# Memory attention: the sample group's scores of four heads in four column groups, keys by batch

## The chip, the cores and the metric

The kernel runs on one core of a Trainium2 chip. Its time is the device time of one execution in microseconds (us), lower is better. Three runs of the kernel before are at hand, and one execution was profiled.

## What is computed

One inference step of a two-layer decoder, for a prompt of 512 tokens and for a sample group of 8 batches with 4 tokens each. Either layer is a mixer (layer 0: paged latent attention beside a state-space layer; layer 1: a gated recurrence), then a cross-attention into 256 memory tokens, then a squared-ReLU MLP, each with a residual. The change is in the cross-attention, whose reference is

```python
def mem_attend(hn, k, v, w_q, q_gain, w_o):
    b, L, _ = hn.shape
    q = rms_norm((hn @ w_q).reshape(b, L, MEM_HEADS, MEM_HEAD_DIM), q_gain)
    sc = jnp.einsum('bqhd,bkhd->bhqk', q, k).astype(jnp.float32) * (MEM_HEAD_DIM ** -0.5)
    pr = jax.nn.softmax(sc, axis=-1).astype(v.dtype)
    o = jnp.einsum('bhqk,bkhd->bqhd', pr, v).reshape(b, L, MEM_WIDTH)
    return o @ w_o
```

Here `hn` is the RMS-normalized residual (1024 features), with 4 heads of 128 features. The prompt's keys and values are computed from a memory; those of the sample group come from caches, 256 keys of 4 heads for each of the 8 batches and each layer. `rms_norm` divides by the root of the mean square plus 1e-6.

## The kernel before

The residual is kept feature-major, with 544 columns: 32 of the sample group, then 512 of the prompt. A dense product (`gemm`, helper `mm3`, line 190) takes 128 output features as a chunk, splits weights and activations into a high and a low part, and sums three products in two PSUM banks (`pbig`, two such pairs); four more banks (`psm`) serve everything small.

`mem_attention` runs once per layer. It begins with the layer norm's factor of each token: `rstd_cols` sums the squares in `acc` with a column of ones (tile `pst_m`), and `rstd_bcast` spreads the result over all partitions by products with the identity (`pbc_m`, `pbn_m`), into `rb`. Then comes the query projection, a `gemm` with one chunk for each head (`ps_mq`). Behind each chunk, `ev` multiplies by `rb` into `qT` (tile `mqT`), squares, and sums the squares for the head's own norm; a power on GpSimd makes the factor `r` from that sum plus 128 times the epsilon. The head's factor is applied later, as the scale of the softmax. `after` calls for each chunk the work that can follow: `head_scores` and `head_values` are the prompt's softmax and values, `sample_scores` the scores of the sample group.

`sample_scores(h)` masks the queries of the head, so that those of one batch stand alone in 32 columns (`mqp`). It loads the head's cached keys of four batches at a time (`mkc`, 512 KB), transposes them on TensorE, copies them out (`mkcT`), and multiplies: all eight batches accumulate in 32 rows of the PSUM tile `msS`, those of the head, with the weights in the head's group of 32 of the array's columns (`tile_position`). The rows are copied to `Ss`. Behind the last chunk come the sample group's softmax (`msP`, `msPT`), its values (`msO`: for each batch a load `mvc` of 512 KB, and eight products that go through the four column groups in turn), and the values of the prompt's heads (`mpt` transposes, `mpo` products). The output projection `ps_wmo` follows.

In layer 0 the steps of `fill` (tile `mkv`, with weights `w_mem_k` and `w_mem_v`) compute the other layer's memory keys and values between these; layer 1 has no such work left. `mkc` and `mvc` share the buffers of the tag `mc`, 5 in layer 0 and 8 in layer 1.

The order of the instructions on each engine is made by a planner: it takes instructions by the order of the program and by when, in its own model of the times, their inputs and buffers are ready. So work that stands later in the program is taken earlier where a hole would be. Loads go through the queue of SyncE (SP), in its order. At its head an instruction waits for its buffer, and those behind it wait too.

## Time and profile before

| what | value |
|---|---|
| median of three runs | 2033.66 us (2030.12 to 2038.61) |
| span of the profiled execution, first to last instruction | 2026.1 us |
| its own device time beside the span | not given with the profile; the median of the runs is 7.6 us above the span |
| TensorE matmul busy | 1974.1 us, 97% of the span |
| VectorE, ScalarE, GpSimd busy | 1250.1, 804.1 and 301.8 us |

The profile names an instruction by its line, engine, operation and tiles (out<-in). PE is TensorE, PEld its loading of weights, DVE VectorE, ACT ScalarE, POOL GpSimd, and SPq the queue of SyncE. An exact float32 product stands in the trace as two matmuls. The start of a matmul is recorded; its end is modelled, so that matmuls which follow each other overlap in the rows, and the time that one takes from the next is read from start to start.

### The profile page before, as it was taken

The numbers are of one execution on the slowest core, as the hardware profiler recorded it, in microseconds if no ns is written. First come the engines' busy times: TensorE is split into PE (matmuls) and PEld (weight loads), VectorE is DVE, ScalarE is ACT, GpSimd is POOL, SyncE is SP. The second block draws the span as 40 slices with busy tenths as digits, with TensorE's granted clock in tenths as the row PEclk, the third lists the DMA queues.
The fourth block names the chain that finished last, engine by engine and source line by source line (L and its number), as shares of the span: only waits on it lengthen the run. The fifth ranks groups of instructions, "written<-read, shape, count | busy, mean of one in ns | idle before, by whom it ended". The sixth has DMA issues, their size and how long they took to land.

```text
span 2026.1 us, 40767 instructions
## 1 busy us (share of the span) xinstructions
PE 1974.1 (97%) x16073; PEld 1848.0 (91%) x16073; DVE 1250.1 (62%) x2781; ACT 804.1 (40%) x1749; POOL 301.8 (15%) x400
## 2 busy tenths in 40 slices
PE   8999899999999999999999999999999999999999
PEld 7878699888899889999999999999898699999998
DVE  7988577877785455444434458888953553435353
ACT  4456655555654344222222334445342432212121
POOL 5677400000012112000000110011141010000000
PEclk9999989999999999999999999999989999999999
DMA  6110132122424533333232332323226132333232
GB/s 157 46 52 30 53 88 52 48 69 70 117 92 94 165 127 106 93 87 92 85 93 84 97 90 82 101 86 92 75 75 170 50 105 87 91 86 92 85 93 76
DMA packets 320480, 178.88 MB, mean 88 GB/s; under 512 B 49153, under 2 KB 312418, under 8 KB 320290
## 3 DMA queue, kind: packets, MB, share of 16 engines
q1 hardware_dynamic: 292466, 163.88, 28.2%
q10 hardware_dynamic: 26224, 8.06, 1.7%
q0 software_dynamic: 1600, 4.34, 0.8%
q8 instruction: 127, 2.08, 0.4%
q14 instruction: 63, 0.52, 0.1%
HBM read 166.42 MB, written 9.82 MB: 87 GB/s over the span
## 4 chain that ended last, share of the span: by engine, by line
PE 79%; SPq 3%; DVE 2%; issue 1%; DMA 1%; ACT 1%; POOL 0%; POOLq 0%; ACTq 0%; DVEq 0%
PE ps_dn L190 19%; PE ps_up L190 19%; PE kp L1110 6%; PE ps_wo L190 4%; PE hv L190 3%; PE ps_hq L190 3%; PE ps_hf L190 3%; PE ps_wmo L190 2%; PE ps_hg L190 2%; PE mkv L190 2%; PE ps_mq L190 2%; PE msS L1381 2%; SPq L1002 1%; SPq L976 1%; PE ct L300 1%
## 5 line engine op out<-in xcount | busy, mean ns | idle before, releaser
L190 PE MATMUL ps_up<-actH_f,wH_up 128*128 128x272 f32 x1024 | 211.9, 288 | 0.8 <-DVE mt L1458 0.8
L190 PE MATMUL ps_dn<-hidL,wH_dn 128*128 128x272 f32 x1024 | 211.7, 288 | 0.0
L190 PE MATMUL ps_up<-actH_f,wL_up 128*128 128x272 f32 x1024 | 210.5, 288 | 0.0
L190 PE MATMUL ps_dn<-hidH,wL_dn 128*128 128x272 f32 x1024 | 210.5, 288 | 0.0
L190 PE MATMUL ps_up<-actL_f,wH_up 128*128 128x272 f32 x1024 | 210.5, 287 | 0.0
L190 PE MATMUL ps_dn<-hidH,wH_dn 128*128 128x272 f32 x1024 | 210.0, 287 | 0.0
L1220 DVE TENSOR_TENSOR h<-ps_dn,h 128x544 f32<-128x544 f32 x64 | 46.4, 724 | 221.2 <-PE ps_dn L190 221.2
L165 ACT ACTIVATE wH_dn<-wraw_dn 128x1024 fp32r<-128x1024 f32 x64 | 68.1, 1063 | 255.1 <-PE ps_dn L190 157.9
L165 ACT ACTIVATE wH_up<-wraw_up 128x1024 fp32r<-128x1024 f32 x64 | 68.1, 1063 | 236.1 <-PE ps_up L190 142.7
L190 PEld LDWEIGHTS ps_up<-actH_f,wH_up 128*128 128x128 f32 x1024 | 159.5, 188 | 1.2 <-PE ps_up L190 1.1
L190 PEld LDWEIGHTS ps_dn<-hidL,wH_dn 128*128 128x128 f32 x1024 | 160.5, 188 | 0.1
L190 PEld LDWEIGHTS ps_up<-actL_f,wH_up 128*128 128x128 f32 x1024 | 160.0, 188 | 0.0
L190 PEld LDWEIGHTS ps_dn<-hidH,wL_dn 128*128 128x128 f32 x1024 | 159.5, 188 | 0.0
L190 PEld LDWEIGHTS ps_up<-actH_f,wL_up 128*128 128x128 f32 x1024 | 159.5, 188 | 0.0
L190 PEld LDWEIGHTS ps_dn<-hidH,wH_dn 128*128 128x128 f32 x1024 | 158.9, 188 | 0.0
L1458 DVE TENSOR_TENSOR mt<-ps_up,rb_f 128x544 f32<-128x544 f32 x64 | 46.2, 724 | 168.8 <-PE ps_up L190 168.6
L1113 ACT ACTIVATE sq<-kp 128x256 f32<-128x256 f32 x256 | 97.7, 386 | 77.8 <-PE kp L1110 47.9
L1116 DVE TENSOR_REDUCE ss<-sq 128x4 f32<-128x256 f32 x256 | 104.3, 412 | 13.3 <-ACT sq L1113 10.5
L166 DVE TENSOR_TENSOR wL_up<-wraw_up,wH_up 128x1024 fp32r<-128x1024 f32 x64 | 78.1, 1221 | 11.3 <-ACT wH_up L165 8.6
L1110 PE MATMUL kp<-wk0H,cH 128*128 128x256 f32 x256 | 79.8, 312 | 2.9 <-DVE S L1115 1.9
L166 DVE TENSOR_TENSOR wL_dn<-wraw_dn,wH_dn 128x1024 fp32r<-128x1024 f32 x64 | 78.2, 1222 | 5.8 <-ACT wH_dn L165 3.0
L1110 PE MATMUL kp<-wk0H,cL 128*128 128x256 f32 x256 | 72.7, 284 | 0.0
(734 smaller groups left out, 5227.1 us busy)
## 6 DMA issues: line engine op xcount, KB each, us to landing
wraw_up<-in_w_mlp_up_dram SPq DMA_DIRECT2D x64, 512.0 KB, 4.0
wraw_dn<-in_w_mlp_down_dram SPq DMA_DIRECT2D x64, 512.0 KB, 3.5
cnat<-in_cache_mla_latent_dram SPq DMA_DIRECT2D x128, 128.0 KB, 2.2
mkc<-in_cache_mem_k_dram SPq DMA_DIRECT2D x16, 512.0 KB, 7.3
mvc<-in_cache_mem_v_dram SPq DMA_DIRECT2D x16, 512.0 KB, 3.3
wraw_w_mem_k<-in_w_mem_k_dram SPq DMA_DIRECT2D x8, 512.0 KB, 5.4
wraw_w_mem_v<-in_w_mem_v_dram SPq DMA_DIRECT2D x8, 512.0 KB, 3.5
wraw_wo<-in_w_out_even_dram SPq DMA_DIRECT2D x8, 512.0 KB, 4.2
```

What stands on the lines that cost most here:

```text
L165: i = nc.scalar.activation(H, x, AF.Copy)
L166: sub.tensor_tensor(out=L, in0=x, in1=H.bitcast(F32), op=ALU.subtract)
L190: nc.tensor.matmul(out, x, sl(y), start=first and n == 0, stop=last and n == 2)
L300: self.nc.tensor.transpose(out, in_, self.ident[:p, :p])
L976: return [self.nc.sync.value_load(self.pt[0:1, b * NPG + t:b * NPG + t + 1], min_val=0, max_val=last) for t in range(NPG)]
L1002: load = lambda x, t, src: nc.sync.dma_start(x, src[bass.ds(pg[t], 1), 0].rearrange("o t c -> (o t) c"))
L1110: mm = nc.tensor.matmul(ps[:, :N], x[:, kt], wt[y][:, kt], start=(kt == 0 and n == 0), stop=(kt == 1 and n == 2))
L1113: nc.scalar.activation(sq, ps[:, :256], AF.Square)
L1116: V.tensor_reduce(out=ss[:, t, 4 * hf:4 * hf + 4], in_=sq.rearrange("p (h d) -> p h d", h=4), op=A, axis=AX.X)
L1220: self.nc.vector.tensor_tensor(out=halves(self.h[:, i, :]), in0=ps, in1=halves(self.h[:, i, :]), op=ALU.add)
L1381: nc.tensor.matmul(ps[32 * h:32 * h + 32, :MEM], qp[:, 4 * g + b, :], kcT[:, b, :], start=(g == b == 0), stop=(g == 1 and b == 3), tile_po ...
L1458: nc.vector.tensor_tensor(out=halves(t), in0=ps, in1=halves(rb), op=ALU.mult)
```

## The change

- `sample_scores` is split. `sample_keys(b)` loads the cached keys of one batch with all four heads (512 KB, runs of 2 KB) and transposes them into `mkcT`, of which there are 3 in layer 0 and 6 in layer 1 (`kbufs`). It is called for two batches behind each chunk as long as there are buffers, and for the other batches behind the projection.
- All score products stand behind the projection: for each batch four products, one for each head, in the four column groups. The masked queries of all heads are kept (`mqp`, 4 buffers). The softmax reads the PSUM tile itself, without `Ss`. `head_scores(2)` is called before the scores and no longer behind the softmax.
- The layer norm's factor is no longer applied to the queries, as the head's own norm cancels it but for the epsilon. `layer_norm` makes the epsilon term `en` of each token from the same sums of squares, and `rnorm` adds it. `rb` is gone; `ev` copies, and squares from PSUM.
- The shared buffers `mc` become 4 in layer 0 and 6 in layer 1. The square of the memory keys (`mksq`) takes a buffer of the tag `sq` in the filler.

The rest of the diff takes comments and docstrings out, which moves line numbers.

```diff
@@ -1282,7 +1282,9 @@
                 if wn == "w_mem_v":
                     break
                 for t in range(2):
-                    sq = p.tile([128, MH, MD], F32, name="mksq")
+                    sq = (self.tp.tile([128, NT], F32, tag="sq", name="mksq")[:, :MH * MD] if parts else
+                          p.tile([128, MH * MD], F32, name="mksq"))
+                    sq = sq.rearrange("p (h d) -> p h d", h=MH)
                     ss = p.tile([128, MH], F32, name="mkss")
                     nc.scalar.activation(sq, kr[:, t], AF.Square)
                     nc.vector.tensor_reduce(out=ss, in_=sq, op=ALU.add, axis=AX.X)
@@ -1296,7 +1298,7 @@
             nc.scalar.dma_start(o["mv_p"][l, 0].rearrange("(t p) h d -> p t (h d)", p=128), v)
 
     def mem_attention(self, l, act, acc, kv, P, fill):
-        """Returns the H and L parts of the attention output, feature-major (from P)."""
+
         nc, a = self.nc, self.a
         V, G = nc.vector, nc.gpsimd
         kT, v = kv
@@ -1304,31 +1306,50 @@
         oL = P.tile([128, MH, NT], F32R, name="moL")
         with self.pool(f"matt{l}", bufs=2, side="left") as p:
             qg = self.col(p, a["mem_q_gain"][l], MD, "g_mq2")
-            rb = self.rstd_bcast(self.rstd_cols(acc, D, f"m{l}"), f"m{l}")
             qT = p.tile([128, MH, NT], F32, name="mqT", bufs=1)
             sqs = p.tile([128, MH, NSAMP], F32, name="msqs", bufs=1)
-            Ss = p.tile([128, MEM], F32, name="msS", bufs=1)
-            # batch of each row (head, batch, position)
+
+
+            en = p.tile([128, TT], F32, name="men", bufs=1)
+            kcT, kbufs = {}, 6 if l else 3
+            qps = []
+
             bcol = p.tile([128, NB], F32, name="mbcol", bufs=1)
             V.tensor_reduce(out=bcol, in_=self.ident.rearrange("p (h b s) -> p b h s", h=MH, b=NB), op=ALU.add, axis=AX.XY)
             bm = self.c("bmask").rearrange("p (b n) -> p b n", b=NB)
             rs = []
 
-            def rnorm(ps, n):
+            def layer_norm():
+                ps = self.psm("pst")
+                for t in range(4):
+                    nc.tensor.matmul(ps[:, t:t + 1], acc[:, tok(t)], self.ones, start=True, stop=True)
+                accr = p.tile([128, MH, NSAMP], F32, name="maccr", bufs=1)
+                G.tensor_copy(accr, acc[:, None, :NSAMP].to_broadcast([128, MH, NSAMP]))
+                nc.tensor.matmul(ps[:, 4:5], accr.rearrange("p h n -> p (h n)"), self.ones, start=True, stop=True)
+                V.tensor_scalar(en, ps[:, :TT], MD * EPS / D, MD * EPS * EPS, op0=ALU.mult, op1=ALU.add)
+
+            def rnorm(ps, c, n):
                 r = p.tile([128, n], F32, name=f"mr{n}", bufs=4 if n > 1 else 1)
-                V.tensor_scalar(r, ps, MD * EPS, None, op0=ALU.add)
+                V.tensor_tensor(out=r, in0=ps, in1=en[:, c:c + n], op=ALU.add)
                 G.tensor_tensor(out=r, in0=r, in1=self.nhalf[:, :n], op=ALU.pow)
                 rs.append(r)
 
             def ev(i, ps):
-                V.tensor_tensor(out=halves(qT[:, i, :]), in0=ps, in1=halves(rb), op=ALU.mult)
+                V.tensor_copy(halves(qT[:, i, :]), ps)
                 sq = self.tp.tile([128, NT], F32, tag="sq", name="msq")
-                nc.scalar.activation(sq, qT[:, i, :], AF.Square)
+                nc.scalar.activation(halves(sq), ps, AF.Square)
                 G.tensor_copy(sqs[:, i, :], sq[:, :NSAMP])
+                if i == 0:
+                    layer_norm()
                 pss = self.psm("mss")
                 for t in range(4):
                     nc.tensor.matmul(pss[:, t:t + 1], sq[:, tok(t)], self.ones, start=True, stop=True)
-                rnorm(pss[:, :4], 4)
+                rnorm(pss[:, :4], 0, 4)
+                qp = p.tile([128, NB, 32], F32, name="mqp", bufs=MH)
+                V.scalar_tensor_tensor(out=qp, in0=qT[:, i, None, :NSAMP].to_broadcast([128, NB, 32]), scalar=qg,
+                                       in1=bm, op0=ALU.mult, op1=ALU.mult)
+                qps.append(qp)
+
             def head_scores(h):
                 r = rs[h]
                 S = self.pbig("mS")
@@ -1361,29 +1382,28 @@
                     nc.tensor.matmul(po, v[:, k, h * MD:(h + 1) * MD], PT[:, k, :], start=(k == 0), stop=(k == 1))
                 self.split(oH[:, h, NSAMP:], oL[:, h, NSAMP:], po)
 
-            # sample group: rows (head, batch, position)
-            def sample_scores(h):
-                qp = p.tile([128, NB, 32], F32, name="mqp")
-                V.scalar_tensor_tensor(out=qp, in0=qT[:, h, None, :NSAMP].to_broadcast([128, NB, 32]), scalar=qg,
-                                       in1=bm, op0=ALU.mult, op1=ALU.mult)
-                ps = self.psm("msS")
-                for g in range(2):
-                    kc = p.tile([128, 8, MD], F32, tag="mc", name="mkc", bufs=8 if l else 5)
-                    nc.sync.dma_start(kc, a["cache_mem_k"][l, 4 * g:4 * g + 4, :, h, :]
-                                      .rearrange("b (t p) d -> p (b t) d", p=128))
-                    kcT = p.tile([128, 4, MEM], F32, name="mkcT")
-                    for x in range(2):
-                        pk = self.psm("mkc")
-                        for y in range(4):
-                            self.transpose(pk[:, y * 128:(y + 1) * 128], kc[:, 4 * x + y, :])
-                        self.copy(kcT[:, 2 * x:2 * x + 2, :].rearrange("p x n -> p (x n)"), pk)
-                    for b in range(4):
-                        nc.tensor.matmul(ps[32 * h:32 * h + 32, :MEM], qp[:, 4 * g + b, :], kcT[:, b, :],
-                                         start=(g == b == 0), stop=(g == 1 and b == 3),
+
+            def sample_keys(b):
+                kc = p.tile([128, 2, MH * MD], F32, tag="mc", name="mkc", bufs=6 if l else 4)
+                kT_ = kcT[b] = p.tile([128, MH, MEM], F32, name="mkcT", bufs=kbufs)
+                nc.sync.dma_start(kc, a["cache_mem_k"][l, b].rearrange("(t p) h d -> p t (h d)", p=128))
+                for x in range(2):
+                    pk = self.psm("mkc")
+                    for y in range(2):
+                        h = 2 * x + y
+                        for t in range(2):
+                            self.transpose(pk[:, y * MEM + t * 128:y * MEM + t * 128 + 128],
+                                           kc[:, t, h * MD:(h + 1) * MD])
+                    self.copy(kT_[:, 2 * x:2 * x + 2, :].rearrange("p x n -> p (x n)"), pk)
+
+            def sample_scores(ps, b0, n):
+                for b in range(b0, b0 + n):
+                    for h in range(MH):
+                        nc.tensor.matmul(ps[32 * h:32 * h + 32, :MEM], qps[h][:, b, :], kcT[b][:, h, :],
+                                         start=(b == 0), stop=(b == NB - 1),
                                          tile_position=(0, 32 * h), skip_group_check=True)
-                self.copy(Ss[32 * h:32 * h + 32], ps[32 * h:32 * h + 32, :MEM])
-
-            def sample_softmax():
+
+            def sample_softmax(Ss):
                 st = p.tile([128, 3], F32, name="msst")
                 V.tensor_reduce(out=st[:, 0:1], in_=Ss, op=ALU.max, axis=AX.X, negate=True)
                 V.tensor_tensor(out=st[:, 0:1], in0=st[:, 0:1], in1=r_s, op=ALU.mult)
@@ -1402,7 +1422,7 @@
                 os = p.tile([128, MD], F32, name="mos", bufs=1)
                 for b in range(NB):
                     po = self.psm("msO")
-                    vc = p.tile([128, 2, MH * MD], F32, tag="mc", name="mvc", bufs=8 if l else 5)
+                    vc = p.tile([128, 2, MH * MD], F32, tag="mc", name="mvc", bufs=6 if l else 4)
                     nc.sync.dma_start(vc, a["cache_mem_v"][l, b].rearrange("(t p) h d -> p t (h d)", p=128))
                     for t in range(2):
                         for h in range(MH):
@@ -1420,7 +1440,9 @@
             def after(ch):
                 if ch > 1:
                     head_scores(ch - 2)
-                sample_scores(ch)
+                for b in (2 * ch, 2 * ch + 1):
+                    if b < kbufs:
+                        sample_keys(b)
                 if ch == 3:
                     head_values(0)
 
@@ -1428,11 +1450,18 @@
             self.gemm(a["w_mem_q"][l], KT, 0, MH, act, ev, f"mq{l}", after=after)
             pss = self.psm("mss")
             nc.tensor.matmul(pss[:, :1], sqs.rearrange("p h n -> p (h n)"), self.ones, start=True, stop=True)
-            rnorm(pss[:, :1], 1)
+            rnorm(pss[:, :1], 4, 1)
             r_s = rs[MH]
-            PT = sample_softmax()
+            head_scores(2)
+            ps = self.psm("msS")
+            for b in range(0, NB, kbufs):
+                n = min(kbufs, NB - b)
+                if b:
+                    for x in range(b, b + n):
+                        sample_keys(x)
+                sample_scores(ps, b, n)
+            PT = sample_softmax(ps[:, :MEM])
             next(fill, None)
-            head_scores(2)
             next(fill, None)
             head_values(1)
             next(fill, None)
```

## Rows read from the trace of the kernel before

**Rows 1.** The page: busy time of the engines; the ended-last chain by line.
```profile
PE 1974.1 (97%) x16073; PEld 1848.0 (91%) x16073; DVE 1250.1 (62%) x2781; ACT 804.1 (40%) x1749; POOL 301.8 (15%) x400
...
PE ps_dn L190 19%; PE ps_up L190 19%; PE kp L1110 6%; PE ps_wo L190 4%; PE hv L190 3%; PE ps_hq L190 3%; PE ps_hf L190 3%; PE ps_wmo L190 2%; PE ps_hg L190 2%; PE mkv L190 2%; PE ps_mq L190 2%; PE msS L1381 2%; SPq L1002 1%; SPq L976 1%; PE ct L300 1%
```

**Rows 2.** Windows: stretch, length, busy of PE, PEld, DVE, ACT, POOL, clock, DMA.
```profile
659.39:703.96 44.57, 44.19 (x319) 37.89 (x318) 16.71 (x32) 13.25 (x25) 7.83 (x9) 1.00 0.59 166
703.96:759.52 55.56, 55.27 (x468) 44.24 (x466) 34.53 (x73) 29.50 (x67) 7.76 (x7) 1.00 0.39 131
1521.32:1567.03 45.71, 44.34 (x319) 37.84 (x317) 17.21 (x32) 12.44 (x25) 7.93 (x9) 1.00 0.61 165
1567.03:1612.72 45.69, 41.81 (x320) 27.76 (x318) 22.36 (x54) 16.74 (x43) 1.88 (x3) 0.96 0.16 52
```

**Rows 3.** Waits of PE, 659:760, then 1521:1613: us in total, times, longest.
```profile
PE ps_mq L190 <- DVE mqT L1324: 0.4, 1, 0.4
...
PE msPT L300 <- ACT msP L1391: 1.3, 1, 1.3
PE ps_mq L190 <- DVE mqT L1324: 1.2, 1, 1.2
```

**Rows 4.** The chain in layer 0, in order of time: start, us, what.
```profile
682.18 1.84 PE msS L1381 x8
...
687.92 0.98 PE msS L1381 x4
```

**Rows 5.** Timeline of matmuls, then of weight loads, in the paged attention.
```profile
322.76 1.94 PE L1144 MATMUL pv<-cnat,Pm 128*32 128x257 f32 x32
324.63 0.62 PE L1146 MATMUL pv<-lat,Pm 32*32 32x257 f32 x2
...
322.76 1.46 PEld L1144 LDWEIGHTS pv<-cnat,Pm 128*32 128x32 f32 x32 [0.16 <-ACT sq L1113]
```

**Rows 6.** Timeline of PE in layer 0, the sample group's values.
```profile
738.09 1.95 PE L1409 MATMUL msO<-mvc,msPT 128*32 128x128 f32 x64
739.98 0.39 PE L190 MATMUL mkv<-wH_w_mem_v,memH 128*128 128x256 f32 x1
```

**Rows 7.** Timeline of PE in layer 0, the layer norm's spreading.
```profile
671.89 1.05 PE L276 MATMUL pbc_m<-ident,r_m 128*128 128x128 f32 x8
...
673.20 0.39 PE L190 MATMUL ps_mq<-actH_m,wH_mq 128*128 128x272 f32 x1
```

**Rows 8.** Timeline of DVE in layer 1, behind the last chunk.
```profile
1567.23 0.72 DVE L1324 TENSOR_TENSOR mqT<-ps_mq,rb_m 128x544 f32<-128x544 f32 x1 [0.50 <-PE ps_mq L190]
...
1568.47 0.48 DVE L1367 SCALAR_TENSOR_TENSOR mqp<-mqT,g_mq,ctab 128x256 f32<-128x256 f32 x1
```

**Rows 9.** Tile views of `mkc` and `mvc`: ns min/median/max, first and last start.
```profile
L1372 SPq DMA_DIRECT2D mkc<-in_cache_mem_k_dram x16: 368/1647/3838, 656.1 to 1530.9; - x16
...
L147 DVE COPY mkcT<-mkc x16: 684/692/692, 679.5 to 1581.0; 128x512 f32<-128x512 f32 x16
...
L1406 SPq DMA_DIRECT2D mvc<-in_cache_mem_v_dram x16: 367/368/445, 695.3 to 1581.5; - x16
```

**Rows 10.** Waits of SP's queue, 640:760.
```profile
SPq L1406 <- PE mkc L300: 20.1, 5, 6.7
```

**Rows 11.** The page, loads: engine, count, KB each, median us to landing.
```profile
mvc<-in_cache_mem_v_dram SPq DMA_DIRECT2D x16, 512.0 KB, 3.3
wraw_w_mem_k<-in_w_mem_k_dram SPq DMA_DIRECT2D x8, 512.0 KB, 5.4
```

**Rows 12.** Timeline of PE in layer 1's tail.
```profile
1585.20 1.12 PE L1361 MATMUL mpo<-mPT,mv 128*128 128x512 f32 x2
...
1590.56 2.07 PE L1361 MATMUL mpo<-mPT,mv 128*128 128x512 f32 x2 [0.58 <-ACT mPT L149]
...
1600.24 0.75 PE L190 MATMUL ps_wmo<-moH,wH_wmo 128*128 128x272 f32 x4
```

**Rows 13.** Groups by line: busy us, mean ns of one, idle before.
```profile
L1381 PEld LDWEIGHTS msS<-mkcT,mqp 128*32 128x32 f32 x128 | 11.8, 109 | 12.3 <-issue 1.2 <-ACT msq L1326 0.7 <-DVE mst L1339 0.3
```

## Prediction

> **What bounds the kernel now.** I read the page first: TensorE is busy for 1974.1 us, 97% of the span, and the chain that ended last is made almost wholly of TensorE lines; `msS`, the line that this change rewrites, is 2% of it [rows 1]. So TensorE's time is the kernel's time wherever TensorE has no hole. Has it holes at the two places that the change touches? The windows view, cut at the last matmul of each layer's query projection, answers. Layer 0 runs from 659.39 to 759.52, and TensorE is busy in 44.19 of 44.57 and in 55.27 of 55.56 us. Layer 1 runs from 1521.32 to 1612.72 and shows 44.34 of 45.71, then 41.81 of 45.69 us at a mean clock of 0.96 [rows 2]. Layer 0 is limited by TensorE alone (it has the other layer's memory keys and values, tile `mkv`, as filler); layer 1 nearly so, with 3.9 us of waits in its tail behind the projection. The waits view names the waits: in layer 0 0.4 us for `mqT`; in layer 1 1.2 us for `mqT` and, the longest of the tail, 1.3 us for `msP` [rows 3].
>
> **Sample scores.** Each of the 32 products of a layer is recorded as two matmuls of 256 columns, 64 in all. Today one head's products follow each other in one group of 32 columns of the array. In the chain a run of 8 takes 1.84 us, a run of 4 0.98 [rows 4]: 0.215 for each further matmul, about 0.12 for going in and out. Layer 0 has 3 runs of 8 and 10 of 4, 3 x 1.84 + 10 x 0.98 = 15.3 us; layer 1 has 2 and 12, 15.4 us.
>
> Afterwards consecutive products go to the four column groups in turn. No row has this product in that order, but two have its like. `pv` rotates the groups with 257 columns: 32 matmuls from 322.76 to 324.63, 1.87 us, 0.058 each [rows 5]. `msO` rotates with 128 columns: 64 from 738.09 to 739.98, 0.030 each [rows 6]. `pv` is the nearest: 64 x 0.058 = 3.7 us a layer in one run. If each batch stands alone, there are seven breaks more at 0.12, 4.5 us. I take 3.8. **Gain 11.6 us a layer, bounds 10.8 and 11.7.**
>
> The weight loads could speak against it. In the `pv` run 32 loads are done in 1.46 us, inside the 1.87 us of the matmuls [rows 5], so they add nothing there. The Trainium skill ("TensorE: Matmul & The Clock Gate", Part 3, "The mechanism") states that a weight load overlaps matmuls in flight only when it goes to another row group. Here all four groups use the same rows, and by that rule the loads would stand in the open; the `pv` rows disagree.
>
> **Layer norm of the queries.** Today `pst_m` (10 matmuls) feeds `r_m`, which 10 more matmuls, `pbc_m` and `pbn_m`, spread over the partitions, from 671.89 to 673.20: 1.3 us a layer [rows 7]. The first chunk's evacuation waits for that, and so does the third chunk's bank: the 0.4 and 1.2 us for `mqT` [rows 3]. All of this goes. The new `layer_norm` has ten matmuls in the place of those of `pst_m`: nothing. Its copy on GpSimd and its step on VectorE are hidden by the projection, in which these engines are busy for 7.8 and 16.7 of 44.6 us [rows 2]; without that cover a wait like today's, 1.2 us. **Gain 1.7 us in layer 0, 2.5 in layer 1.**
>
> **Evacuations.** The multiply by `rb` becomes a copy of the same size, the square reads the bank instead of `qT`, and four copies of `msS` and two of `rb` a layer are gone: nothing on TensorE, which works on beside them. It matters behind the last chunk. Today `mqT`, a weight part and `mqp` follow from 1567.23 to 1568.95, 1.7 us [rows 8]; afterwards they stand ahead of all scores, since no batch can be scored before head 3's queries are there. So what moves is this: today half of the `msS` runs lie inside the projection, then none does. TensorE has other work meanwhile (prompt heads, key transposes, in layer 0 the filler).
>
> **Keys by batch.** The transposes and copies are as many as before. The loads keep their 512 KB but with runs of 2 KB, as `mvc` has them: an issue takes SP 0.37 instead of 1.65 us [rows 9], 10 us a layer less in its queue. Against that, the buffers that `mkc` and `mvc` share fall from 5 to 4 in layer 0 and from 8 to 6 in layer 1, and only 3 or 6 transposed batches fit. In layer 0 keys 3 to 7 can be copied only after scores have freed a buffer, so behind the projection; the value loads wait for key buffers, and behind them in SP's queue stand the weights of `mkv` and `wmo`, for which the filler waits. SP's value loads wait 20.1 us for `mkc` already [rows 10], yet TensorE has 0.3 us of idle in that stretch [rows 2], because the filler covers it. New waits of layer 0: from 0 to 4 us (one load that starts when it is needed, 0.37 of issue and 3.3 to land [rows 9, 11]); I take 1.
>
> In layer 1 the value loads 6 and 7 can start only when values 0 and 1 have been used, behind the softmax of the samples, where today all eight are there. Two prompt heads' values can stand beside them, each with two `mpo` pairs of 1.1 us [rows 12] and its transposes. The tail loses cover, too: of its 41.8 us of work 7.7 are `msS` (6 runs of 4, 1 of 8), and 3.8 come back. It also pays a spell at the lower of the two clock levels: the pair of `mpo` at 1590.56, behind a wait of 0.58, takes 2.07 us, where the pair at 1585.20 takes 1.12 [rows 12]. The mean of 0.96 over 45.69 us is 3.7 us at half the clock, 1.8 us lost. New waits of layer 1: from 0 to 6 us (today's 3.9 a second time, and one such spell more); I take 3, near the middle, because TensorE still has 41.8 - 7.7 + 3.8 = 37.9 us of work there against a sample chain of 21 us: 1.7 of evacuation, 3.8 of scores, 0.7 for the last key copy [rows 9], and the 15.0 us that pass today from the end of `msS` at 1585.20 to the first `wmo` matmul at 1600.24 [rows 12].
>
> **The sum.** Layer 0: 11.6 + 1.7 - 1 = 12.3. Layer 1: 11.6 + 2.5 - 3 = 11.1. Together 23.4 us. What follows either place runs at TensorE's pace and simply comes earlier. The profiled execution's span is 2026.1 us; what lies around it is not in the page, and the median of the three runs, 2033.66, is 7.6 above it. Span 2026.1 - 23.4 = 2002.7, time 2002.7 + 7.6 = **2010.3 us**. With the bounds: the low score cost, no new wait and the old clock spell gone, 2 x 11.7 + 4.2 + 1.8 = 29.4, time 2004; the high score cost and all new waits, 2 x 10.8 + 4.2 - 10 = 15.8, time 2018.
>
> **The rivals.**
> - Waits eat half (0.15). One layer overruns its bound: layer 0 uses its filler up early, or the tail of layer 1 goes by its chains, 5 us more. For it: SP's long waits and fewer buffers. Against it: 99% busy in layer 0. Gain 10 to 16 us, 2018 to 2023.
> - The columns don't run side by side, with the loads in the open (0.02). A load of `msS` has 0.109 us [rows 13]; 64 add 7.0 us to the 3.8, so the gain is 4.6 a layer instead of 11.6: 2 x 4.6 + 4.2 - 4 = 9.4, 2024. The rotating runs speak against it [rows 5, 6]. This is what the rule cited above would give (the Trainium skill, "TensorE: Matmul & The Clock Gate", Part 3, "The mechanism").
> - No change that shows (0.10). Each layer gets one new wait as long as the gain: the first value product waits for its load, which stood behind a key buffer. SP's longest such wait is 6.7 us [rows 10], and two loads behind each other take 6.6, 13.3 in all. For it: only a freed buffer starts a value load. Against it: `msO` comes 34 us behind the projection in layer 0. Time 2024 to 2044.
> - Slower (0.05). SP's queue is in order: value loads that wait for key buffers stand ahead of the weights of `mkv`, the filler cannot start, and TensorE stops in layer 0 behind the scores. From 23.4 us of such a stop on, the kernel is slower; all eight weight loads behind it, 5.4 us each for those of the keys [rows 11], are 43 us, less the gain 20, 2053.
>
> The rest, 0.68, is the forecast with its bounds, 2004 to 2018. A change under 0.5% (10 us) can't be told from none in this kernel, whose three runs span 8.5 us. Faster by more: 0.68 + 0.15 = 0.83; within: 0.02 + 0.10 = 0.12; slower: 0.05. Eight times in ten: 2004 to 2021, which leaves out the last three rivals and the worst of the first.
>
> **What would show it.** In the new profile: `msS` in runs of 8 or more at about 0.06 us each, 3.8 us a layer; no `pbc_m` or `pbn_m`; layer 0 from the first `ps_mq` to the first `ps_wmo` matmul 88 us instead of 100.1; layer 1's stretch 80 instead of 91.4. It would be wrong if `msS` rows stayed 0.2 us apart, if TensorE waited for `mkcT`, `mvc` or a weight part for more than 5 us in either stretch, or if the clock of layer 1's tail fell for longer than the 3.7 us of now.

## The result and the profile after

| kernel | median of its runs | ratio to the kernel before, 95% interval |
|---|---|---|
| before | 2031.89 us (2023.94 to 2038.61, 4 runs) | |
| after | 2009.63 us (2008.20 to 2011.25, 4 runs) | 0.9909 [0.9891, 0.9928] |
| after, a second time, beside the experiments | 2011.87 us (2006.30 to 2015.30, 6 runs) | 0.9922 [0.9906, 0.9939] |

The changed kernel is faster by 0.6 to 1.1%. The profiled execution took 2010.12 us, and its span is 2008.4: 17.7 us less than the span before.

The page of the changed kernel, the same two lines as [rows 1]:

```profile
PE 1952.4 (97%) x16053; PEld 1840.0 (92%) x16053; DVE 1249.2 (62%) x2773; ACT 801.1 (40%) x1743; POOL 299.9 (15%) x398
...
PE ps_dn L190 19%; PE ps_up L190 19%; PE kp L1110 6%; PE ps_wo L190 4%; PE hv L190 3%; PE ps_hq L190 3%; PE ps_hf L190 3%; PE ps_mq L190 2%; PE ps_wmo L190 2%; PE ps_hg L190 2%; PE mkv L190 2%; SPq L1002 1%; SPq L976 1%; PE ct L300 1%; PE hatt L1654 1%
```

TensorE is 21.7 us less busy, and `msS`, 2% of the chain that ended last before, is no longer among its listed lines. Where did the time go? I cut each layer from its first `ps_mq` matmul to the first `ps_up` matmul of the MLP behind it. (The prediction cut layer 0 at the first `ps_wmo` matmul. By that mark it went from 100.1 to 95.6 us, 658.59 to 754.15, where 88 was forecast. But the mark flatters the change: four `mpo` matmuls, 1.3 us, that stood ahead of it now stand behind it.) The windows view of PE alone (length, busy, granted clock, DMA share and rate), first the kernel before, then the changed one; in each, layer 0 and layer 1:

```profile
659.39:784.57 125.18, 124.47 (x980) 1.00 0.47 143
1521.32:1630.74 109.42, 104.17 (x779) 0.98 0.40 113
```

```profile
658.59:781.21 122.62, 118.83 (x969) 0.97 0.44 144
1516.77:1612.54 95.77, 89.98 (x770) 0.98 0.40 129
```

Layer 1 gives 13.7 us, layer 0 only 2.6: there TensorE has 3.8 us of holes where it had 0.7, and its clock, 1.00 before, has a mean of 0.97.

The scores themselves do what was forecast. Timeline of PE in layer 1, behind the projection:

```profile
1561.08 2.80 PE L1402 MATMUL msS<-mkcT,mqp 128*32 128x256 f32 x48
1563.81 2.00 PE L300 MATMUL mkc<-ident,mkc 128*128 128x128 f32 x16
1565.74 1.48 PE L1402 MATMUL msS<-mkcT,mqp 128*32 128x256 f32 x16
1568.76 0.44 PE L300 MATMUL msPT<-ident,msP 128*128 128x128 f32 x2 [1.54 <-ACT msP L1411]
...
1578.38 0.65 PE L1429 MATMUL msO<-mvc,msPT 128*32 128x128 f32 x16 [1.70 <-DMA mvc<-in_cache_mem_v_dram]
```

48 matmuls from 1561.08 to 1563.81 are 0.057 us each, where [rows 4] had 0.215 for a further one. (The last row is the wait for a late value load that the prediction expected in this tail.) Layer 0's scores are as quick in one run of 24, and then they come in pieces:

```profile
706.40 1.50 PE L1402 MATMUL msS<-mkcT,mqp 128*32 128x256 f32 x24
707.83 0.66 PE L300 MATMUL mkc<-ident,mkc 128*128 128x128 f32 x4
...
715.60 0.64 PE L1402 MATMUL msS<-mkcT,mqp 128*32 128x256 f32 x8
716.17 0.66 PE L300 MATMUL mkc<-ident,mkc 128*128 128x128 f32 x4
716.75 0.63 PE L1402 MATMUL msS<-mkcT,mqp 128*32 128x256 f32 x4
717.31 0.44 PE L300 MATMUL mkc<-ident,mkc 128*128 128x128 f32 x2
```

Read from start to start: the 24 take 1.43 us, the eight 0.57, the four 0.56. There are nine such short pieces in layer 0 (one of two, one of six, one of eight, six of four) and each takes 0.55 to 0.57. With the 24 that is 6.45 us; the prediction had 3.8, and 4.5 if each batch stood alone.

The hole is in layer 0, behind the last matmul of the projection. PE's timeline there, and then ScalarE's:

```profile
690.70 1.89 PE L1357 MATMUL mS<-mkT,mqT 128*128 128x256 f32 x8
695.47 1.85 PE L1346 MATMUL mss<-ones,msq 128*128 128x1 f32 x8 [2.88 <-ACT msq L1340]
697.18 1.95 PE L300 MATMUL mpt<-ident,mP 128*128 128x128 f32 x8
698.92 3.58 PE L1357 MATMUL mS<-mkT,mqT 128*128 128x256 f32 x8
```

```profile
690.65 1.06 ACT L165 ACTIVATE wH_w_mem_k<-wraw_w_mem_k 128x1024 fp32r<-128x1024 f32 x1 [2.27 <-PE ps_mq L190]
691.62 3.29 ACT L168 ACTIVATE memH<-memT,g_ms 128x256 fp32r<-128x256 f32 x8
694.81 0.61 ACT L1340 ACTIVATE msq<-ps_mq 128x544 f32<-128x544 f32 x1
```

TensorE waits 2.88 us for `msq`, the square of the last query chunk. ScalarE could have begun it at 691.7, but ahead of it in its queue stand the eight `memH` splits of the filler, 3.29 us. (The Trainium skill, "PSUM — Partial Sum Buffer", "Engine vs sequencer instructions", says that ScalarE's queue is strictly first in, first out; these rows agree.) Behind the wait everything takes nearly twice as long: eight `mS` matmuls 3.58 us, where eight took 1.89 before it. The windows view of PE shows why:

```profile
695.50:702.30 6.80, 6.80 (x25) 0.50 0.12 44
```

The granted clock is 0.50 in this stretch, the lower of the two levels (1.2 instead of 2.4 GHz), though TensorE is busy in all of it; what came just before is the idle time.

The same order stood on ScalarE in the kernel before. Its timelines of ScalarE and of PE:

```profile
704.87 3.29 ACT L168 ACTIVATE memH<-memT,g_ms 128x256 fp32r<-128x256 f32 x8
708.06 0.65 ACT L1326 ACTIVATE msq<-mqT 128x544 f32<-128x544 f32 x1
```

```profile
705.77 1.05 PE L1381 MATMUL msS<-mkcT,mqp 128*32 128x256 f32 x4
706.76 0.44 PE L300 MATMUL mkc<-ident,mkc 128*128 128x128 f32 x2
707.12 1.05 PE L1381 MATMUL msS<-mkcT,mqp 128*32 128x256 f32 x4
708.10 0.87 PE L300 MATMUL mkc<-ident,mkc 128*128 128x128 f32 x6
708.82 1.89 PE L1336 MATMUL mS<-mkT,mqT 128*128 128x256 f32 x8
710.54 0.95 PE L1330 MATMUL mss<-ones,msq 128*128 128x1 f32 x8
```

Before, scores by head and key transposes filled 705.77 to 710.54, and `mss` had nothing to wait for. After, no batch can be scored until head 3's queries are there. So my theory: the change took away the work that covered a late square (lost cover), and the clock doubled the damage. The rival: TensorE lacks work there anyhow, so the wait only moves; or it is the loads and SP's queue that hold layer 0 up.

### The profile page after: what moved, and what is told of

It is laid out like the page before. It is cut to its first block, busy times and chain, and to the rows that moved or that the text cites. A ratio compares the mean times of both kernels' runs of the same rounds, so it can differ in the third digit from the quotient of the medians.

```text
span 2008.4 us, 40691 instructions
## 1 busy us (share of the span) xinstructions
PE 1952.4 (97%) x16053; PEld 1840.0 (92%) x16053; DVE 1249.2 (62%) x2773; ACT 801.1 (40%) x1743; POOL 299.9 (15%) x398
## 4 chain that ended last, share of the span: by engine, by line
PE 79%; SPq 3%; DVE 2%; issue 1%; DMA 1%; ACT 1%; POOL 0%; POOLq 0%; ACTq 0%; DVEq 0%
PE ps_dn L190 19%; PE ps_up L190 19%; PE kp L1110 6%; PE ps_wo L190 4%; PE hv L190 3%; PE ps_hq L190 3%; PE ps_hf L190 3%; PE ps_mq L190 2%; PE ps_wmo L190 2%; PE ps_hg L190 2%; PE mkv L190 2%; SPq L1002 1%; SPq L976 1%; PE ct L300 1%; PE hatt L1654 1%
```

## The experiments

Each stretch below is cut as above. Each ratio is to runs of the kernel before that were timed beside it (medians 2028.64 us for e1 to e4, 2026.25 for e5 to e8, 2027.15 for e9 to e12); each stretch is read from one execution. The stretch is the finer measure: the first `ps_mq` matmul of layer 0 starts anywhere from 658.0 to 663.4 us in these executions, although no edit touches what lies ahead of it, and the medians carry that.

| kernel | median, us | ratio to before, 95% interval | layer 0 | clock there | layer 1 | clock there |
|---|---|---|---|---|---|---|
| before | | | 125.18 | 1.00 | 109.42 | 0.98 |
| after | 2009.63 | 0.9909 [0.9891, 0.9928] | 122.62 | 0.97 | 95.77 | 0.98 |
| e5, after again | 2011.87 | 0.9922 [0.9906, 0.9939] | 122.63 | 0.97 | 95.80 | 0.98 |
| e1, square first | 2006.00 | 0.9894 [0.9878, 0.9911] | 115.67 | 1.00 | 95.88 | 0.98 |
| e2, the same in before | 2032.42 | 1.0018 [1.0008, 1.0028] | 129.28 | 1.00 | 107.88 | 1.00 |
| e3, scores by head | 2023.88 | 0.9975 [0.9963, 0.9986] | 127.38 | 0.97 | 102.86 | 0.97 |
| e4, whole batches | 2006.82 | 0.9896 [0.9880, 0.9913] | 118.83 | 0.97 | 95.59 | 0.98 |
| e6, e1 and e4 | 2004.63 | 0.9893 [0.9875, 0.9910] | 114.17 | 1.00 | 95.62 | 0.98 |
| e7, old norm | 2015.93 | 0.9951 [0.9935, 0.9966] | 122.06 | 1.00 | 98.51 | 0.98 |
| e8, buffers 8 and 4 | 2011.12 | 0.9921 [0.9908, 0.9935] | 121.83 | 0.97 | 96.07 | 0.98 |
| e9, e1 with old norm | 2009.48 | 0.9904 [0.9879, 0.9928] | 118.09 | 1.00 | 99.11 | 0.98 |
| e10, wait filled | 2008.12 (one run) | | 118.78 | 1.00 | 95.69 | 0.98 |
| e11, keys in four loads | 2010.86 | 0.9919 [0.9894, 0.9945] | 122.45 | 0.97 | 95.80 | 0.98 |
| e12, e6 and a new tail | 1999.34 | 0.9851 [0.9831, 0.9871] | 114.61 | 1.00 | 90.39 | 1.00 |

**e5: the changed kernel again.** Unaltered, beside e6 to e8.

> The changed kernel unaltered, for a like comparison with the edits timed beside it. Both theories: 2009 to 2011 by its first measurement, ratio to the kernel before 0.989 to 0.993. If the lost cover is the cause, its 2.9 us wait for msq and the 6.83 us spell at half clock behind it in layer 0 are there again; if they were a chance of one execution, they are not.

Its stretches are those of its first execution within 0.03 us, with the same wait of 2.9 us for `msq` and a clock of 0.97 in layer 0: not chance. Its ratio is 0.1 points nearer to 1, within the intervals; its median, 2011.87, lies above the 2009 to 2011 that were expected.

**e1: the square ahead of the splits.** `issue_after` keeps the instructions inside it behind the named one in their engine's queue. The edit, in the filler and in the evacuation:

```diff
+            with self.tc.issue_after(self.last_sq) if parts else nullcontext():
-            for k in range(KT):
-                self.split(H[:, k, :], L[:, k, :], self.memT[:, k, :], g[:, k:k + 1])
+                for k in range(KT):
+                    self.split(H[:, k, :], L[:, k, :], self.memT[:, k, :], g[:, k:k + 1])
...
-                nc.scalar.activation(halves(sq), ps, AF.Square)
+                self.last_sq = nc.scalar.activation(halves(sq), ps, AF.Square).ins
```

> One edit to the changed kernel: in layer 0 the eight memH splits of the filler are queued on ScalarE behind the square of the last query chunk instead of ahead of it. Theory (lost cover): the square (msq) then starts about 3 us earlier, the 2.9 us for which the mss matmuls wait go, and so does the spell at half clock behind that wait (6.83 us, about 3.4 us lost). 4 to 6 us off the changed kernel's 2009.6, so 2003.5 to 2005.5; no wait for msq over 0.5 us in layer 0. Rival (TensorE has nothing else there in any case): the wait only moves to the filler's first products, which need memH; time 2008 to 2011, and the clock still falls.

Layer 0 lost 6.95 us, a little more than the 4 to 6 expected, although the median, 2006.00, lies 0.5 above the range that was expected of it. ScalarE's timeline with the edit, and PE's:

```profile
692.90 0.62 ACT L1341 ACTIVATE msq<-ps_mq 128x544 f32<-128x544 f32 x1
693.42 3.30 ACT L168 ACTIVATE memH<-memT,g_ms 128x256 fp32r<-128x256 f32 x8
```

```profile
691.88 1.89 PE L1358 MATMUL mS<-mkT,mqT 128*128 128x256 f32 x8
693.60 1.02 PE L1347 MATMUL mss<-ones,msq 128*128 128x1 f32 x8
694.49 1.07 PE L300 MATMUL mpt<-ident,mP 128*128 128x128 f32 x8
```

The wait is gone and did not move: TensorE had enough else to do until `memH` was there.

**e2: the same edit in the kernel before.**

> The same edit on the kernel before. Theory (lost cover): the memH block stood ahead of msq there too, but score and key work of the first heads covered it, so the edit is worth nothing there: within 1.5 us of the kernel before. Rival (the order on ScalarE always cost TensorE this): 4 to 6 us less than the kernel before, and then the changed order of the scores has nothing to do with it.

It gained nothing there, so the order on ScalarE was no loss before the change. It cost something: layer 0 is 4.1 us longer, and the run 0.08 to 0.28% slower. The waits view of PE in layer 0 has a new row:

```profile
PE mkv L190 <- ACT mP L1345: 2.2, 1, 2.2
```

There the filler's first products came next, and now they waited for ScalarE. Before, splits first was the right order; after the change, square first is. (Layer 1's 1.5 us less, with no spell at half clock, is not of the edit's making: it touches layer 0 alone.)

**e10: the wait filled.** Twelve products that nobody reads stand between the projection and `mss`; ScalarE's order stays as changed. The planner of the order also put head 0's two `mpo` products ahead of the filler behind it.

```diff
                 pss = self.psm("mss")
+                d = None
+                if i == 3 and not l:
+                    for x in range(12):
+                        d = nc.tensor.matmul(pss[:, 128:256], self.ident, self.ident, start=True, stop=True).ins
+                with self.tc.issue_after(d) if d else nullcontext():
+                    for t in range(4):
+                        m = nc.tensor.matmul(pss[:, t:t + 1], sq[:, tok(t)], self.ones, start=True, stop=True)
```

> The changed kernel with twelve products of the identity by itself (128 columns each, about 2.8 us by the 0.24 us of a like product of mS) queued in layer 0 between the last projection matmul and the mss matmuls that wait for msq, whose order on ScalarE stays. Their result is read by nobody. They prolong nothing if they fit into the wait. Theory (the idle time brings the clock down): the wait for msq falls under 0.4 us, the granted clock stays at 1.00 through layer 0, and the eight mpt and eight mS matmuls behind it take 1.0 and 1.9 us instead of 1.95 and 3.58; layer 0's stretch is 3 to 3.5 us shorter though the same time passes before mss. Rival (the clock falls for another cause): the spell at half clock stays, and the stretch is within 1 us.

PE's timeline, and the windows view of what follows:

```profile
692.74 2.84 PE L1348 MATMUL mss<-ident 128*128 128x128 f32 x24
695.41 1.89 PE L1363 MATMUL mS<-mkT,mqT 128*128 128x256 f32 x8
697.50 1.05 PE L1351 MATMUL mss<-ones,msq 128*128 128x1 f32 x8 [0.20 <-ACT msq L1340]
698.41 1.07 PE L300 MATMUL mpt<-ident,mP 128*128 128x128 f32 x8
699.32 1.89 PE L1363 MATMUL mS<-mkT,mqT 128*128 128x256 f32 x8
```

```profile
697.50:704.30 6.80, 6.80 (x48) 1.00 0.12 41
```

From the projection's last matmul to `mss` as much time passes as in the changed kernel (692.74 to 697.50, against 690.70 to 695.47), and layer 0 is 3.84 us shorter all the same. 0.6 of that is a wait of `msO` for a value load, which the changed kernel has and e10 has not; the other 3.2 are near half of the 6.8 us at half clock. So the idle time brought the clock down, and the spell cost somewhat more than the wait itself: of e1's 6.95 us about 3.3 are the clock, 2.9 the wait, and 0.7 scores that came in fewer pieces (5.77 instead of 6.45).

**e3: scores head by head.** The two loops of the scores are exchanged; loads, buffers and norm stay.

```diff
-                for b in range(b0, b0 + n):
-                    for h in range(MH):
+                for h in range(MH):
+                    for b in range(b0, b0 + n):
```

> One edit to the changed kernel: the sample scores of the batches at hand are made head by head (one column group at a time) instead of batch by batch (the four groups in turn); loads, buffers and layer norm stay as changed. Theory (the turns are the gain): msS matmuls are back at about 0.215 us each in place of 0.057, 8 to 10 us more in layer 0 where runs are short, 10 more in layer 1: 18 to 20 us slower than the changed kernel, near the kernel before. Rival (the gain came from shorter issues on SP, fewer copies and the layer norm): under 5 us slower, and the msS matmuls stay near 0.06 us.

The timeline of PE in layer 1:

```profile
1567.41 8.05 PE L1402 MATMUL msS<-mkcT,mqp 128*32 128x256 f32 x48
1575.39 2.00 PE L300 MATMUL mkc<-ident,mkc 128*128 128x128 f32 x16
```

The same 48 matmuls on the same data now take 7.98 us, 0.166 each, instead of 2.73. The stretches are 4.8 and 7.1 us longer than the changed kernel's, and 0.14 to 0.37% is all that is left of the gain over before: the turns are the gain, as the theory had it. The size was expected too high, because the edit undoes the turns only in part: the first eight matmuls of this run start about 0.215 us apart, as before, but further on, and more so in layer 0, the planner still puts products of two heads in turn, and two then start in that time. Of the 11.9 us by which the two stretches grew, 8.0 are the scores (18.6 us in both layers instead of 10.7); the rest are waits and a changed order. Longer runs by themselves are worth little: 64 matmuls at 0.215 are 13.8 us a layer (an estimate) against the 15.3 and 15.4 of before.

The weight loads are as many in either order. In the changed kernel's run of 48 they are done inside the 2.73 us of the matmuls:

```profile
1561.08 2.32 PEld L1402 LDWEIGHTS msS<-mkcT,mqp 128*32 128x32 f32 x48
```

So the quick order does not have them in the open. That is against the rule of the Trainium skill that the prediction weighed ("TensorE: Matmul & The Clock Gate", Part 3, "The mechanism").

**e4: each batch in one run.**

```diff
-                    for h in range(MH):
-                        nc.tensor.matmul(ps[32 * h:32 * h + 32, :MEM], qps[h][:, b, :], kcT[b][:, h, :],
...
+                    def one(h):
...
+                    with self.tc.issue_after(one(MH - 1).ins):
+                        for h in range(MH - 1):
+                            one(h)
```

> One edit to the changed kernel: the products of heads 0 to 2 of a batch are queued behind that of head 3, so that a batch's scores are made in one run of eight matmuls in all four column groups, not in two halves as each key copy ends. Theory (broken runs): layer 0's msS falls from 6.45 to about 4.3 us and its filler is broken less often, 2 to 3.5 us less than the changed kernel; layer 1, where the runs are whole already, stays. Rival (the halves fill holes that would otherwise be idle): the msS time falls, and the stretch of layer 0 stays within 1 us, because TensorE then waits for the second copy.

Layer 0's scores are one run of 24 and five of eight, 4.28 us, and its stretch is 3.8 us shorter. 2.2 of that are the scores and 0.6 the wait of `msO` for a value load, which is gone; most of the other 1.0 lies in the key transposes and the filler, which are broken less often. TensorE waited for nothing new. The wait for `msq` and its spell are still there, so this loss is separate from e1's.

**e6: both.**

> Two edits to the changed kernel together: the filler's memH splits behind the last chunk's square on ScalarE, and each batch's sample scores in one run of eight. Alone they took 6.9 and 3.8 us from layer 0's stretch (projection to the first ps_up matmul). Theory (two separate losses): they add but for about 0.7 us, since the first edit alone already lowers msS from 6.45 to 5.77: 9 to 11 us less stretch in layer 0, about 2000 to 2002. Rival (both win the same hole in layer 0's TensorE work): no more than the better one alone, 2003.5 to 2006.

Layer 0 is 8.45 us shorter, less than the 9 to 11 expected, and the time is that of the rival. They are two losses, since together they beat either, but the sum falls 2.3 us short of the 10.74 of the two alone. 0.7 was foreseen; 1.1 more is idle time of TensorE, above all a wait of 1.2 us of `msO` for a value load, which a quicker layer 0 reaches sooner and which neither edit alone has.

**e7 and e9: the old layer norm, without and with e1's edit.** In both, `pst_m`, `pbc_m` and `pbn_m` are back:

```diff
+            rb = self.rstd_bcast(self.rstd_cols(acc, D, f"m{l}"), f"m{l}")
...
-                V.tensor_copy(halves(qT[:, i, :]), ps)
+                V.tensor_tensor(out=halves(qT[:, i, :]), in0=ps, in1=halves(rb), op=ALU.mult)
...
-                if i == 0:
-                    layer_norm()
```

> One part of the change undone: the layer norm of the queries through the spread factor (r_m, pbc_m, pbn_m, multiply by rb) is back, the batch order of keys and scores stays. Theory (the prediction's term): 1.7 us more in layer 0 and 2.5 more in layer 1, of which 1.3 each is the ten matmuls: 3.5 to 5 us slower than the changed kernel. Rival (the norm was hidden in the projection anyway): only the matmuls, 2.6 us at most, and no wait for mqT over 0.2 us. A second rival: the third chunk's longer wait moves work of the tail, and the change of either layer has the other sign.

> Two edits to the changed kernel: the memH splits stand behind the last chunk's square (as in the first experiment), and the layer norm of the queries is back in its old form (as in the run that undid it alone, where layer 0's stretch from the projection to the first ps_up matmul was 122.06 against 122.62, and the wait for msq 1.2 instead of 2.9 us). Theory (the norm's gain in layer 0 was real, and the wait for msq ate it, because TensorE reached that wait 1.7 us earlier): without that wait the old norm costs its 1.7 us again, layer 0 is 117.0 to 117.8 against 115.68 of the first experiment, layer 1 is 98.5. Rival (the norm was hidden in layer 0): 115.2 to 116, layer 1 98.5.

Layer 1 shows the term as predicted: 2.7 us longer, 1.2 of it the wait for `mqT` as in [rows 3]. In layer 0 the old norm costs nothing by itself, it is even 0.6 us quicker. PE's two longest waits there in e7:

```profile
PE mss L1335 <- ACT msq L1331: 1.2, 1, 1.2
PE msO L1418 <- DMA mvc<-in_cache_mem_v_dram: 0.9, 1, 0.9
```

The wait for `msq` is 1.2 instead of 2.9: what the new norm saves on TensorE it spends waiting for ScalarE's late square, and behind the longer wait comes the spell at half clock, which e7 has not (clock 1.00). That e7 is quicker by no more than 0.6 goes with 1.9 us of waits, for `moH`, `mkT` and `mPT`, that the changed kernel has not. The second rival expected the other sign in one of the layers, and layer 0 has it, but through `msq` and not through the third chunk's wait. With the square first, the norm is worth 118.09 - 115.67 = 2.4 us in layer 0 as well, 0.3 more than the top of what was expected; layer 1 is 0.6 above the 98.5 expected, with a wait for a value load of 2.3 us where e7 has 1.8. So the first rival of e7, hidden in the projection, falls: the gain was real, and eaten.

**e8: eight load buffers, four key buffers in layer 1.**

```diff
-            kcT, kbufs = {}, 6 if l else 3
+            kcT, kbufs = {}, 4 if l else 3
...
-                kc = p.tile([128, 2, MH * MD], F32, tag="mc", name="mkc", bufs=6 if l else 4)
+                kc = p.tile([128, 2, MH * MD], F32, tag="mc", name="mkc", bufs=8 if l else 4)
```

> One size changed in the changed kernel: in layer 1 eight buffers for key and value loads instead of six, paid with four transposed key batches instead of six. Theory (the value loads 6 and 7 wait for buffers): the 1.7 us wait of msO for its load in layer 1 goes, and with it perhaps 1.7 us of the half-clock spell behind the sample chain: 1 to 3 us less. Rival (the tail goes by the sample chain, and the wait only moves to msP or moH): within 1 us; or the scores, now in two parts, come later, and the tail is 1 to 3 us longer.

The wait for value loads went, and layer 1 is 0.3 us longer: the rival. The scores now come in a run of 32, four of four and one of 16, between the last keys' transposes, and `msOT` waits 1.0 instead of 0.5.

**e11: each batch's keys in four loads.**

```diff
-                nc.sync.dma_start(kc, a["cache_mem_k"][l, b].rearrange("(t p) h d -> p t (h d)", p=128))
+                for h in range(MH):
+                    nc.sync.dma_start(kc[:, :, h * MD:(h + 1) * MD],
+                                      a["cache_mem_k"][l, b, :, h].rearrange("(t p) d -> p t d", p=128))
```

> One part of the change undone: each batch's cached keys are loaded by four DMAs of one head each, in runs of 512 bytes as before, into the same buffer. SP then issues for longer, about 1.3 us more a batch by the rows of before. Theory (the loads' issue time is hidden, as the prediction costed it): layer 0's and layer 1's stretches within 1 us of the changed kernel, 122.6 and 95.8. Rival (SP's queue is what the value loads and the filler's weights wait for): 3 to 10 us more in layer 0, with a longer wait of msO for its load.

An issue now takes SP 0.47 us, and there are four for a batch, where the changed kernel has one of 0.44. Both stretches are the changed kernel's within 0.2 us: SP's shorter issues are worth nothing, and its queue does not hold layer 0 up.

**e12: layer 1's tail.** To e6, in layer 1 alone:

```diff
                 V.reciprocal(st[:, 2:3], st[:, 1:2])
+                if l:
+                    head_values(1)
                 ps = self.psm("msPT")
...
                 for b in range(NB):
+                    if l and b == 6:
+                        head_values(2)
                     po = self.psm("msO")
```

(The two calls that stood behind are left to layer 0.)

> The kernel with the first two edits (memH splits behind the last square, batch scores in whole runs; layer 1's stretch 95.62 there), and in layer 1 two heads of the prompt moved: head 1's transposes and values stand ahead of the transposes of msP, and head 2's between the sixth and the seventh batch of sample values. Theory (layer 1's tail still has the waits that the prediction named, 1.5 us for msP and 1.7 for the value loads 6 and 7, and work to cover them): both go, 3 to 4 us less, and 1.7 more if the spell at half clock goes with them: layer 1's stretch 90.5 to 92.5, time near 2001. Rival (the tail goes by its chains): the waits turn up at other instructions, the stretch is within 1 us of 95.6.

PE's timeline:

```profile
1563.33 1.98 PE L1383 MATMUL mpo<-mPT,mv 128*128 128x512 f32 x4
1565.82 0.44 PE L300 MATMUL msPT<-ident,msP 128*128 128x128 f32 x2 [0.50 <-ACT msP L1415]
1567.05 2.83 PE L1437 MATMUL msO<-mvc,msPT 128*32 128x128 f32 x96 [0.80 <-DVE msPT L1423]
1569.81 1.09 PE L300 MATMUL mpt<-ident,mP 128*128 128x128 f32 x8
1571.21 1.12 PE L1383 MATMUL mpo<-mPT,mv 128*128 128x512 f32 x2 [0.31 <-ACT mPT L149]
1572.27 1.19 PE L1437 MATMUL msO<-mvc,msPT 128*32 128x128 f32 x28
```

Nothing in layer 1 waits for a value load any more, the wait for `msP` is 0.5, and the spell at half clock is gone: layer 1 is 5.2 us shorter than in e6. TensorE's holes there shrank by 3.3 us; that the spell went for that reason is likely but not shown, since e2 has none either, with the waits of the kernel before. This version, 1.3 to 1.7% under the kernel before, is faster than both kernels.

## Why the prediction was right, and where it was not

The forecast of 2010.3 us met 2009.63, but that is luck: two errors of some 6 us cancel in it. The sum gave 23.4 us, and the span fell by 17.7. On the other side, the prediction put 7.6 us between span and time, the distance to the median of other executions; the profiled run after has 2010.12 - 2008.4 = 1.7. With 1.7 the same sum would have given 2004.4, and its bounds 1998 to 2012: the range would still have held the result, the number not. The interval of the ratio, 15 to 22 us of 2031.89, holds the 17.7 and not the 23.4; that of the second measurement, 12 to 19 us of 2026.25, does too.

- **The turns.** Right in kind and price: 0.057 us a matmul against the 0.058 taken from `pv`. Layer 1: 15.4 to 2.73 + 1.48 = 4.2 us, a gain of 11.2 (predicted 11.6). Layer 0: 8.9, under the lower bound of 10.8. That bound broke off the runs at whole batches, and a copy of keys holds two heads, so half batches were scored as their copies came (e4). By the prediction's price a piece of four would take 4 x 0.058 + 0.12 = 0.35 us, and it took 0.56; a whole batch of eight took 0.57, near the 0.58 that the price gives.
- **The loads beside the matmuls.** Right: 48 of them in 2.32 us, inside the matmuls' 2.73 (e3).
- **The layer norm.** 1.7 and 2.5 predicted; 2.4 (e9 against e1) and 2.7 (e7). In layer 0 as changed, nothing of it arrived.
- **Keys by batch, and SP's issues.** Costed at nothing, and SP's issues are worth nothing (e11). The fewer copies, the softmax that reads the bank, the earlier `head_scores(2)` and layer 0's four load buffers were not undone one by one.
- **New waits of layer 1.** I took 3 of 0 to 6. The wait for a value load came as described, 1.7 us, though for the last load alone, and the waits of the tail grew by 1.7 in all. But TensorE's other work in the layer took about as much less, and the clock was no worse: 11.2 + 2.7 = 13.9, measured 13.7, so 0.2 net. That these two would cancel was not foreseen. What the tail had lost in waits and clock could be had back (e12).
- **New waits of layer 0: the step that failed.** I took 1 of 0 to 4 and looked for them on SP's queue, at loads and weights, which were innocent (`msO` 0.6 instead of 0.3). The wait came on ScalarE, 2.9 us, and with it a spell at half clock, worth about 3.3, that I had priced for layer 1 alone. The prediction named the cause without drawing it out: half of the `msS` runs lie inside the projection today and none will; "TensorE has other work meanwhile". It did not ask what those runs covered. The two rows of ScalarE and of PE side by side, shown above for the kernel before, would have answered: `msq` ends at 708.7, the last projection matmul starts some 5 us earlier, and all between but the `mS` matmuls was work that the change moves or shrinks.

In sum for layer 0: 8.9 and 2.4 gained, 2.9 and 3.3 lost, leaves 5.1; measured 2.6. Of the other 2.5, 0.3 is the load wait. Most of the rest lies in products that come in more pieces. Read from start to start, `msO` takes 4.65 us instead of 3.91, in seven runs instead of three; in e10, where no spell at half clock blurs it, `mkv` takes 25.05 instead of 24.48 and `mpo` 6.56 instead of 5.72. The key transposes are not among it (7.22 instead of 7.52). Which part of the change breaks these products up was not tested.

The first rival, one layer beyond its bound, describes what layer 0 did, though neither of its two mechanisms: the filler was not used up, and the tail of layer 1 did not give way.

## What to carry to other kernels

When a change takes work out of a place, look up on every other engine's queue what that work was covering, not only at the transfers that the change touches; an order that was free before can be the new wait. A hole on TensorE can have two prices, its own length and a spell at half clock behind it, so filling or removing a hole of a few microseconds can be worth twice its length. Products that use only some of the array's columns should come in whole turns through all column groups, and in runs long enough that going in and out doesn't dominate.

## What was not expected of the hardware

A short run of `msS` matmuls takes 0.55 to 0.57 us whether it has two, four, six or eight, so that a run of four that uses two column groups is no cheaper than one of eight that uses four; 24 take 1.43 and 48 take 2.73. And a single idle time of 2.88 us, in a stretch in which TensorE is otherwise busy in full, was followed by 6.8 us at the lower clock. All profiles with that wait of 2.9 us have it (after, e3, e4, e5, e8, e11: clock 0.97 in layer 0), and none of those in which the square came first (e1, e6, e9, e12) nor that in which the wait was filled (e10). The hole of 2.2 us in e2 and that of 1.2 in e7 have no such spell behind them.
